# Norms of q and k in DeltaNet heads: squares by channel and a product with ones in place of transposes

## The chip, the cores and the metric

The kernel runs on one core of a Trainium2 chip. A core has five engines that run their own instruction streams and wait for each other by semaphores: TensorE (matrix products into the PSUM banks), VectorE, ScalarE, GpSimd and SyncE, which here only issues DMAs. The metric is the device time of one execution in microseconds, lower is better. The time before is the median of three runs.

## The reference

One decoder layer for 256 tokens of 2048 channels in float32. One projection `u @ w_in` feeds two token mixers, stick-breaking attention and a gated DeltaNet, each with 16 heads of 128 channels; gates merge them, and a SwiGLU network follows. The change concerns the norms of the DeltaNet's q and k:

```python
def _l2norm(x):
    return x * lax.rsqrt(jnp.sum(x * x, axis=-1, keepdims=True) + EPS)
...
qkv_b = jax.nn.silu(_causal_depthwise_conv(qkv_b, conv_w[l]))
qb, kb, vb = jnp.split(qkv_b, (D_GDN_K, 2 * D_GDN_K), axis=-1)
qb = _l2norm(_heads(qb, GDN_HEADS, GDN_K_DIM)) * (GDN_K_DIM ** -0.5)
kb = _l2norm(_heads(kb, GDN_HEADS, GDN_K_DIM))
...
o_b = _gated_delta_rule(qb, kb, vb, g, beta)
```

The delta rule solves, for each chunk and head, a unit lower triangular system made of `beta * k k^T * decay`. The kernel never writes normalised q or k: the inverse roots of the sums of squares enter as factors, by token, into that system and into the output's scaling.

## The kernel before

**Projections.** `run_jobs` walks through jobs of 512 output columns. For every 256 rows of a weight it loads a tile `raw`, makes a rounded high part `wh` (ScalarE, line 304) and the rest `wl` (VectorE, line 310), and TensorE forms three products for each part: high by high, high by low, low by high (tile `acc`). The q, k and v projections of the DeltaNet come out with channels on the partitions (`chan`), each product 256 columns wide; other projections have products 512 columns wide.

**DeltaNet chains.** The 16 heads are worked on in four groups of `HG` = 4, one chain each (`gdn_chain`). A convolution chain (`conv_chain`) makes the tiles `gq`, `gk`, `gv` (in the code `qT`, `kT`, `vT`: 128 channels by 4 heads by 256 tokens) with a Silu at its end. The tokens are worked on in two blocks of 128, the digit in the step's name. `gdn_slots` gives each step a slot in a table, and `paced` issues the TensorE part of a step at its slot and the evacuations it returns some slots later. A slot passes with each pump of the job loop, between the products of the projections. The steps that matter here:

- G and D: the decay matrix, with an Exp on ScalarE.
- K0, K1 (slots 1 and 4), T0, T1 (slots 10 and 14): four transposes each, of k or q, to have tokens on the partitions; then, one slot later, four squares on ScalarE with a sum along the channels (`accum_out`), two slots later EPS and the root on VectorE and GpSimd (`root`), two slots later the factors (`coef`, for k). K0 also copies the transposed k to `k0`, which step S0 reads at slot 53.
- KK0, KK1 (slots 7 and 13): k k^T, scaled into the system `L` with the factors. From KK1 on, the inverse of the diagonal blocks is made by substitution on VectorE (`gather`, `enter`, `stages`, `leave`), then scattered by ScalarE (`scatter`) and turned by VectorE (`turn`).
- X and Q (from slot 32): products that grow the inverse from blocks of 16 to 32 to 64, each handed between TensorE, ScalarE and VectorE. Y, W, U, S, O, R, E: the rest of the inverse, the state and the outputs, and the output scaling of the chain.

**Order.** The framework plans each engine's order from the traced program: of the work that is ready by its own estimates it takes what was written first. So projections that are written behind a step run ahead of it while it is not ready; engines then execute their orders strictly. The step X0 is written in the same slot as B1, and in the trace of the second chain it runs about 20 us behind it. PSUM has eight banks, four with the tag `acc` and four with the tag `ms`; the chain's steps take theirs from `ms` (`bank`). Tiles of the tag `h2` (five) hold the squares.

Of the kernel before, what the change touches and what calls it, by code (L numbers as in the profile page):

```python
# [11 lines left out]
AF = mybir.ActivationFunctionType  # L12
ALU = mybir.AluOpType
# [9 lines left out]
HG = 4  # L23
NG = H // HG
DFF = 5632
EPS = 1e-6
# [71 lines left out]
def body(tc, cst, x, c, w_mod, b_mod, norm1_w, w_in, q_norm_w, k_norm_w, conv_w, a_log, dt_bias,  # L98
         o_norm_w, p_a, p_b, w_out, norm2_w, w_gate, w_up, w_down, out, dbg=None):
    nc = tc.nc  # L100
    ctx = ExitStack()
    x, w_mod, b_mod, w_in, p_a, p_b, w_out, w_gate, w_up, w_down, out, conv_w = (
        t[0] for t in (x, w_mod, b_mod, w_in, p_a, p_b, w_out, w_gate, w_up, w_down, out, conv_w))
# [7 lines left out]
    def bank(name, tag="ms"):  # L111
        return ps.tile([P, 512], F32, tag=tag, name=name)
# [4 lines left out]
    def mm(o, lhsT, rhs, start=True, stop=True):  # L117
        nc.tensor.matmul(o, lhsT=lhsT, rhs=rhs, start=start, stop=stop, skip_group_check=True)  # L118

    def tt(o, a, b, op):  # L120
        nc.vector.tensor_tensor(out=o, in0=a, in1=b, op=op)  # L121

    def stt(o, a, s, b, op0, op1, **kw):
        nc.vector.scalar_tensor_tensor(out=o, in0=a, scalar=s, in1=b, op0=op0, op1=op1, **kw)  # L124

    def act(o, i, f, **kw):
        nc.scalar.activation(out=o, in_=i, func=f, **kw)

    def f32(t):
        return t.bitcast(F32)  # L130
# [4 lines left out]
    ident, ones = cs0[:, 0:P], cs0[:, P:2 * P]  # L135
# [3 lines left out]
    def tr(o, i):  # L139
        nc.tensor.transpose(o, i, ident)  # L140
# [31 lines left out]
    def rsqrt(o, i):  # L172
        nc.gpsimd.tensor_tensor(out=o, in0=i, in1=half[:, 0:o.shape[-1]], op=ALU.pow)
# [377 lines left out]
    def bc(v, n=P):  # L551
        return v.unsqueeze(2).to_broadcast([P, v.shape[1], n])

    def mid(v, n):
        return v.unsqueeze(1).to_broadcast([P, n, v.shape[1]])

    def four(b):
        return b.rearrange("p (h n) -> p h n", h=4)
# [23 lines left out]


    def gdn_slots():
        at = {"K0": 1, "K1": 4, "D0": 5, "KK0": 7, "D1": 11, "KK1": 13}
        fill = {"T0": 10, "T1": 14, "A0": 16, "B0": 22, "A1": 26, "B1": 32, "V0": 40, "V1": 44}
        out = [(t, o) for o, t in {**at, **fill}.items()] + [(0, "G0"), (6, "G1")]
        for i in range(len(LEVELS)):
            b = 13 + BD + 2 * HOP * i
            out += [(b, "X0"), (b + HOP, "Q0"), (b + LAG, "X1"), (b + LAG + HOP, "Q1")]  # L590
        b += 2 * HOP
        out += [(b, "Y0"), (b + HOP, "W0"), (b + LAG, "Y1"), (b + LAG + HOP, "W1"), (b + 2 * HOP, "U0"), (b + 3 * HOP, "S0"),
                (b + 3 * HOP + 1, "O0"), (b + 4 * HOP, "S1"), (b + 4 * HOP + 1, "R1"), (b + 5 * HOP, "U1"), (b + 6 * HOP, "O1"),
                (b + 6 * HOP + 4, "E1")]
        return sorted(out)
# [16 lines left out]
    def gdn_chain(g, tl):  # L612
        while tl.get("ready", 0) < 2:
            yield
        qT, kT, vT = (tl[n] for n in "qkv")
# [13 lines left out]
        k0 = four(wB[:, 3, 512:1024])  # L629
        rr = tp.tile([P, 2, 16], F32, tag="rr", name="rr", bufs=2)  # L630
# [6 lines left out]
        h2 = lambda n, dt=F32: four(tp.tile([P, 512], dt, tag="h2", name=n, bufs=H2))  # L637
# [3 lines left out]
        hold = {}  # L641
# [11 lines left out]
        ph = lambda b, h: b[:, h * P:(h + 1) * P]  # L653
# [60 lines left out]
        def step(op, c):  # L714
            ts = slice(c * P, (c + 1) * P)
# [3 lines left out]
            if op == "G":  # L719
                Gh, Gl = hold["G", c] = h2("Gh", F32R), h2("Gl", F32R)  # L720

                def dve(o, gx):
                    return lambda: tt(o, mid(mk["triL"], HG), bc(f32(gx)[:, c, hs]), ALU.mult)
                return [(1, dve(Gh, gth)), (2, dve(Gl, gtl))]
            if op in "KT":
                src, n0 = (kT, 8) if op == "K" else (qT, 0)
                b = bank("pb_" + op)
                for h in range(HG):
                    tr(ph(b, h), src[:, h, ts])
                n4 = slice(n0 + c * HG, n0 + (c + 1) * HG)  # L730

                def squares():
                    if op == "K" and c == 0:
                        nc.scalar.copy(out=k0, in_=four(b))
                    j = h2("sqj")
                    for h in range(HG):
                        n = n0 + c * HG + h
                        act(j[:, h], ph(b, h), AF.Square, accum_out=rr[:, 0, n:n + 1])

                def root():  # L740
                    nc.vector.tensor_scalar(out=rr[:, 0, n4], in0=rr[:, 0, n4], scalar1=EPS, scalar2=None, op0=ALU.add)
                    rsqrt(r[:, n4], rr[:, 0, n4])

                def coef():
                    if op == "K":
                        tt(brk[:, s4], beta[:, c, hs], rk[:, s4], ALU.mult)
                        stt(nbrk2[:, s4], brk[:, s4], -1.0, rk[:, s4], ALU.mult, ALU.mult)
                        if c:
                            tt(bge, nbrk2[:, 4:8], egc[:, 1, hs], ALU.mult)
                return [(1, squares), (3, root), (5, coef)]  # L750
            if op == "D":
                Gh, Gl = hold.pop(("G", c))
                b = bank("pb_d")
# [3 lines left out]
            if op == "V":  # L757
                while tl["ready"] < 3:
                    pump_conv()
                b = bank("pb_v")  # L760
# [7 lines left out]
            if op == "KK":  # L768
                b = bank("pb_kk")
# [10 lines left out]
                n = -(-(BW - 2) // BST)  # L780
# [5 lines left out]
            if op == "A":  # L786
                b = bank("pb_qk")
# [3 lines left out]
            if op == "B":  # L791
                b = bank("pb_at")
# [3 lines left out]
            if op in "XQ":  # L796
# [3 lines left out]
                b = bank("pb_" + op)[:, 0:256]  # L800
# [21 lines left out]
            if op == "Y":  # L822

                b = bank("pb_X")
# [11 lines left out]
            if op == "W":  # L836
                b = bank("pb_Q")
# [8 lines left out]
            if (op, c) == ("U", 0):  # L846
                b = bank("pb_u0")
# [7 lines left out]
            if (op, c) == ("S", 0):  # L855
                b = bank("pb_s")
# [4 lines left out]
            if (op, c) == ("O", 0):  # L861
                b = bank("pb_o0")
# [9 lines left out]
            if (op, c) == ("S", 1):  # L872
                b = bank("pb_ks")
# [8 lines left out]
            if op == "R":  # L882
                b = bank("pb_qs")
# [4 lines left out]
            if (op, c) == ("U", 1):  # L888
                b = bank("pb_u1")
# [4 lines left out]
            if (op, c) == ("O", 1):  # L894
                b = bank("pb_o1")
                for h in range(HG):
                    mm(ph(b, h), attT[:, HG + h], hold["u1"][:, h])
                o1 = hold["o"]

                def squares():  # L900
                    j = h2("sqj")
                    for h in range(HG):
                        act(j[:, h], o1[:, h], AF.Square, accum_out=sso[:, 0, HG + h:HG + h + 1])
                return [(1, lambda: tt(o1, four(b), o1, ALU.add)), (3, squares)]
# [12 lines left out]
            def apply(h):  # L917
# [7 lines left out]
                [(5 + h, apply(h)) for h in range(HG)]  # L925

        yield from paced(gdn_slots(), step)

    mk = {}
# [30 lines left out]
    for g in GROUPS:  # L960
# [8 lines left out]
        for i in range(3):  # L969
            n = "qkv"[i]  # L970
# [439 lines left out]
```

## Time and profile before

| What | Value |
|---|---|
| Median of three runs | 2052.79 us (2048.81 to 2055.16) |
| The profiled execution | 2056.12 us, span from first to last instruction 2054.1 us |
| TensorE busy | 1983.1 us, 97% |
| VectorE busy | 1386.4 us, 67% |
| ScalarE busy | 1064.9 us, 52% |
| GpSimd busy | 108.9 us, 5% |
| Mean granted TensorE clock | 0.991 |

In the profile's rows PE is TensorE's matmuls, DVE is VectorE, ACT is ScalarE, POOL is GpSimd. Matmuls are pipelined: one lasts longer than the distance to the next, so the cost of a matmul in a stream is read from the distance between two starts. L12 is line 12 of the kernel; L118 and L140 are the helpers for products and transposes, L127 that for activations. The clock is a share of TensorE's full 2.4 GHz; at 0.50 it runs at 1.2 GHz.

### The profile page before, as it was taken

Reading aid. Unit: us, or ns where it says so; the run is one execution under the profiler, and the core shown is the slowest. Engines: PE = TensorE matmul, PEld = TensorE weight load, DVE = VectorE, ACT = ScalarE, POOL = GpSimd, SP = SyncE. Lnnn points to the kernel's source line nnn. Section 1 sums busy time; section 2 is a strip of 40 time slices with the busy share of each in tenths; the row PEclk is TensorE's granted clock in tenths of the full one; section 3 lists DMA queues with packets and bytes.
Section 4 is the critical chain, followed back from the end, with each engine's and each line's share of the span. In section 5 each row is a group of like instructions: output and inputs, shape, how many; then the busy total and the mean of one; then the engine's idle time right before and its main releaser. Section 6 shows DMA issues by size and latency. Waiting matters only on the chain.

```text
span 2054.1 us, 29271 instructions
## 1 busy us (share of the span) xinstructions
PE 1983.1 (97%) x11097; PEld 1720.7 (84%) x11097; DVE 1386.4 (67%) x1846; ACT 1064.9 (52%) x1766; POOL 108.9 (5%) x141
## 2 busy tenths in 40 slices
PE   1999999999999999999999999999999999999998
PEld 1899999897888888888888888788888888888887
DVE  4986979877676667447776877676775555556554
ACT  3346676776666667443454445554455334445432
POOL 4311011010000000000000000000000000000000
PEclk9899999999999999999999999999999999999999
DMA  8995533444776675768797888587875566665564
GB/s 302 386 336 184 160 126 116 125 122 142 240 229 197 223 232 165 222 193 284 253 309 257 301 320 277 178 269 239 268 244 185 195 193 188 188 189 186 186 214 134
DMA packets 208555, 449.72 MB, mean 219 GB/s; under 512 B 16103, under 2 KB 16538, under 8 KB 207902
## 3 DMA queue, kind: packets, MB, share of 16 engines
q1 hardware_dynamic: 198910, 413.25, 62.6%
q0 software_dynamic: 9504, 34.61, 4.5%
q8 instruction: 87, 1.43, 0.3%
q14 instruction: 54, 0.44, 0.1%
HBM read 445.70 MB, written 2.10 MB: 218 GB/s over the span
## 4 chain that ended last, share of the span: by engine, by line
PE 93%; DMA 3%; DVE 2%; issue 1%; ACT 1%; POOL 0%; SPq 0%; DVEq 0%; ACTq 0%; POOLq 0%
PE acc L118 85%; DMA smod<-in_w_mod 1%; DMA crow<-in_conv_w 1%; PE pb_mod L118 1%; PE pb_Q L118 1%; DMA raw<-in_w_in 0%; PE pb_oa L118 0%; PE pb_z L118 0%; PE pb_X L118 0%; DVE wl L121 0%; PE pb_af L118 0%; DVE accb L124 0%; PE pb_o L118 0%; PE pb_u L118 0%; PE pb_tr L140 0%
## 5 line engine op out<-in xcount | busy, mean ns | idle before, releaser
L121 DVE TENSOR_TENSOR wl<-raw,wh 128x1024 fp32r<-128x1024 f32 x648 | 791.8, 1224 | 515.4 <-ACT wh L304 513.8
L304 ACT CAST wh<-raw 128x1024 fp32r<-128x1024 f32 x648 | 680.2, 1050 | 776.7 <-PE acc L118 694.9
L118 PE MATMUL acc<-u,wh 128*128 128x512 f32 x1408 | 494.8, 396 | 0.0
L118 PE MATMUL acc<-u,wl 128*128 128x256 f32 x1408 | 395.3, 281 | 0.0
L118 PEld LDWEIGHTS acc<-u,wh 128*128 128x128 f32 x1408 | 264.2, 188 | 63.1
L118 PE MATMUL acc<-wh,uh 128*128 128x512 f32 x768 | 307.1, 400 | 0.0
L118 PE MATMUL acc<-wl,uh 128*128 128x512 f32 x768 | 300.6, 391 | 0.0
L118 PE MATMUL acc<-wh,ul 128*128 128x512 f32 x768 | 300.1, 391 | 0.0
L118 PEld LDWEIGHTS acc<-u,wl 128*128 128x128 f32 x1408 | 266.1, 189 | 0.2
L118 PE MATMUL acc<-uh,wh 128*128 128x256 f32 x768 | 221.3, 291 | 1.5 <-ACT part L955 1.5
L118 PE MATMUL acc<-ul,wh 128*128 128x256 f32 x768 | 218.8, 286 | 0.0
L118 PE MATMUL acc<-uh,wl 128*128 128x256 f32 x768 | 218.7, 286 | 0.0
L118 PE MATMUL acc<-wh,ff 128*128 128x512 f32 x704 | 216.9, 389 | 0.0
L118 PEld LDWEIGHTS acc<-wl,uh 128*128 128x128 f32 x768 | 144.5, 188 | 30.8
L118 PEld LDWEIGHTS acc<-wh,ul 128*128 128x128 f32 x768 | 144.8, 189 | 27.2
L118 PEld LDWEIGHTS acc<-wh,uh 128*128 128x128 f32 x768 | 144.7, 188 | 26.8
L118 PEld LDWEIGHTS acc<-wh,ff 128*128 128x128 f32 x704 | 132.0, 188 | 27.5
L118 PEld LDWEIGHTS acc<-uh,wh 128*128 128x128 f32 x768 | 148.6, 195 | 2.6 <-ACT part L955 1.7
L118 PEld LDWEIGHTS acc<-ul,wh 128*128 128x128 f32 x768 | 148.6, 193 | 0.6
L118 PEld LDWEIGHTS acc<-uh,wl 128*128 128x128 f32 x768 | 148.0, 193 | 0.4
L118 PE MATMUL acc<-wl,ff 128*128 128x512 f32 x352 | 137.0, 389 | 0.0
L202 DVE SCALAR_TENSOR_TENSOR macc<-wm,cols,macc 128x1024 f32<-128x1024 f32 x92 | 117.7, 1280 | 0.8 <-DMA wm<-in_w_mod 0.6
(289 smaller groups left out, 2269.2 us busy)
## 6 DMA issues: line engine op xcount, KB each, us to landing
raw<-in_w_in SPq DMA_DIRECT2D x286, 512.0 KB, 4.2
wm<-in_w_mod SPq DMA_DIRECT2D x128, 512.0 KB, 5.6
raw<-in_w_gate SPq DMA_DIRECT2D x88, 512.0 KB, 4.5
raw<-in_w_up SPq DMA_DIRECT2D x88, 512.0 KB, 4.4
raw<-in_w_down SPq DMA_DIRECT2D x88, 512.0 KB, 4.3
smod<-in_w_mod POOLq DMA_DIRECT2D x64, 512.0 KB, 11.4
raw<-in_p_a SPq DMA_DIRECT2D x32, 512.0 KB, 4.9
raw<-in_p_b SPq DMA_DIRECT2D x32, 512.0 KB, 5.0
```

Of the source, the lines that this page charges most:

```text
L118: nc.tensor.matmul(o, lhsT=lhsT, rhs=rhs, start=start, stop=stop, skip_group_check=True)
L121: nc.vector.tensor_tensor(out=o, in0=a, in1=b, op=op)
L202: ins = nc.vector.scalar_tensor_tensor(out=acc, in0=t, scalar=cc[:, k:k + 1], in1=acc, op0=ALU.mult, op1=ALU.add)
L304: nc.scalar.copy(out=wh, in_=raws[n])
```

## The change

Instead of transposing k and q and squaring the transposed heads one by one, the squares are taken where the tiles lie, with channels on the partitions: one activation for four heads (new steps N0, N1 for k, M0, M1 for q). The sums over channels are made by TensorE: in steps K and T the squares of each head are the stationary side of a product with one column of ones, whose result has tokens on the partitions, one column for each head. VectorE adds EPS directly from that bank. The transposed k that K0 left for S0 is made by a step of its own, C0, at slot 36. The slots of K0 and K1 go from 1 and 4 to 2 and 5; the root comes one slot after the product, the factors two later.

```diff
-        at = {"K0": 1, "K1": 4, "D0": 5, "KK0": 7, "D1": 11, "KK1": 13}
-        fill = {"T0": 10, "T1": 14, "A0": 16, "B0": 22, "A1": 26, "B1": 32, "V0": 40, "V1": 44}
+        at = {"N0": 0, "K0": 2, "N1": 3, "K1": 5, "D0": 5, "KK0": 7, "D1": 11, "KK1": 13}
+        fill = {"M0": 8, "T0": 10, "M1": 12, "T1": 14, "C0": 36, "A0": 16, "B0": 22, "A1": 26, "B1": 32, "V0": 40, "V1": 44}
...
+            if op in "NM":
+
+                src = kT if op == "N" else qT
+                hold[op, c] = j = h2("sqj")
+                return [(1, lambda: act(j, src[:, :, ts], AF.Square))]
             if op in "KT":
-                src, n0 = (kT, 8) if op == "K" else (qT, 0)
-                b = bank("pb_" + op)
+                n0 = 8 if op == "K" else 0
+                j = hold.pop(("N" if op == "K" else "M", c))
+                b = bank("pb_n")
                 for h in range(HG):
-                    tr(ph(b, h), src[:, h, ts])
+                    mm(b[:, h:h + 1], j[:, h], ones[:, 0:1])
                 n4 = slice(n0 + c * HG, n0 + (c + 1) * HG)
 
-                def squares():
-                    if op == "K" and c == 0:
-                        nc.scalar.copy(out=k0, in_=four(b))
-                    j = h2("sqj")
-                    for h in range(HG):
-                        n = n0 + c * HG + h
-                        act(j[:, h], ph(b, h), AF.Square, accum_out=rr[:, 0, n:n + 1])
-
                 def root():
-                    nc.vector.tensor_scalar(out=rr[:, 0, n4], in0=rr[:, 0, n4], scalar1=EPS, scalar2=None, op0=ALU.add)
+                    nc.vector.tensor_scalar(out=rr[:, 0, n4], in0=b[:, 0:HG], scalar1=EPS, scalar2=None, op0=ALU.add)
                     rsqrt(r[:, n4], rr[:, 0, n4])
...
-                return [(1, squares), (3, root), (5, coef)]
+                return [(1, root), (3, coef)]
+            if op == "C":
+
+                b = bank("pb_K")
+                for h in range(HG):
+                    tr(ph(b, h), kT[:, h, ts])
+                return [(1, lambda: nc.scalar.copy(out=k0, in_=four(b)))]
```

## Rows read from the trace of the kernel before

**Rows 1.** The chain that ended last, shares of the span by engine.

```profile
PE 93%; DMA 3%; DVE 2%; issue 1%; ACT 1%; POOL 0%; SPq 0%; DVEq 0%; ACTq 0%; POOLq 0%
```

**Rows 2.** Windows: length, busy us of PE, PEld, DVE, ACT, POOL, then granted clock.

```profile
185.00:500.00 315.00, 303.26 (x2463) 286.35 (x2462) 262.74 (x622) 220.42 (x548) 31.14 (x37) 0.98 0.43 129
```

**Rows 3.** Timeline of TensorE at step X: start, us, instruction, [idle before].

```profile
243.93 0.45 PE L118 MATMUL pb_X<-gw 128*64 128x64 f32 x8 [1.42 <-issue]
244.31 0.39 PE L118 MATMUL acc<-ul,wh 128*128 128x256 f32 x1
...
329.71 0.70 PE L118 MATMUL pb_X<-gw 128*64 128x64 f32 x8 [2.88 <-ACT gw L127]
...
399.62 0.69 PE L118 MATMUL pb_X<-gw 128*64 128x64 f32 x8 [3.94 <-issue]
...
479.37 0.62 PE L118 MATMUL pb_X<-gw 128*64 128x64 f32 x8 [3.00 <-issue]
```

**Rows 4.** Windows of five microseconds from each X on.

```profile
244.00:249.00 5.00, 4.65 (x52) 4.13 (x53) 4.76 (x16) 4.57 (x13) 0.00 (x0) 1.00 0.09 35
329.70:334.70 5.00, 4.99 (x45) 4.62 (x45) 4.39 (x13) 2.91 (x7) 0.00 (x0) 0.70 0.23 63
399.60:404.60 5.00, 4.97 (x35) 4.66 (x37) 3.69 (x13) 3.50 (x8) 0.00 (x0) 0.52 0.05 17
479.40:484.40 5.00, 5.00 (x33) 3.95 (x35) 3.48 (x10) 2.50 (x5) 0.00 (x0) 0.66 0.32 87
```

**Rows 5.** Timeline of TensorE, first chain, around K0, K1 and KK0.

```profile
195.88 0.60 PE L140 MATMUL pb_K<-cs,gk 128*128 128x128 f32 x4
196.23 0.36 PE L118 MATMUL acc<-uh,wl 128*128 128x256 f32 x1
196.44 0.28 PE L118 MATMUL acc<-uh,wh 128*128 128x256 f32 x1
196.55 0.28 PE L118 MATMUL acc<-ul,wh 128*128 128x256 f32 x1
...
197.26 0.60 PE L140 MATMUL pb_K<-cs,gk 128*128 128x128 f32 x4
...
200.53 1.15 PE L118 MATMUL pb_kk<-gk 128*128 128x128 f32 x8
201.44 0.36 PE L118 MATMUL acc<-uh,wh 128*128 128x256 f32 x1
```

**Rows 6.** Timeline of VectorE: waits ahead of X in chains two to four.

```profile
296.65 0.69 DVE L121 TENSOR_TENSOR part<-acc,part 128x512 f32<-128x512 f32 x1 [0.99 <-PE acc L118]
...
362.36 0.17 DVE L741 TENSOR_SCALAR rr<-rr 128x4 f32<-128x4 f32 x1 [2.91 <-ACT sqj L127]
...
454.09 1.23 DVE L121 TENSOR_TENSOR wl<-raw,wh 128x1024 fp32r<-128x1024 f32 x1 [1.72 <-ACT wh L304]
```

**Rows 7.** Timeline of ScalarE: a cast, the squares of T1, a set for K0, a 512-wide activation.

```profile
235.88 1.05 ACT L304 CAST wh<-raw 128x1024 fp32r<-128x1024 f32 x1 [1.83 <-PE acc L118]
...
298.56 0.28 ACT L127 ACTIVATE sqj<-pb_T 128x128 f32<-128x128 f32 x1
...
439.93 0.30 ACT L127 ACTIVATE sqj<-pb_K 128x128 f32<-128x128 f32 x1
...
440.94 0.53 ACT L127 ACTIVATE gv<-acc,cw 128x256 f32<-128x256 f32 x1
...
446.66 0.63 ACT L127 ACTIVATE gv<-gv 128x512 f32<-128x512 f32 x1
447.20 1.03 ACT L304 CAST wh<-raw 128x1024 fp32r<-128x1024 f32 x1
```

**Rows 8.** Timeline of TensorE: two products of 32 and 16 columns.

```profile
185.36 0.52 PE L118 MATMUL pb_g<-gt,cs 128*128 128x32 f32 x4
185.72 0.36 PE L118 MATMUL acc<-uh,wl 128*128 128x256 f32 x1
```

**Rows 9.** Timeline of TensorE: T1 of the second chain.

```profile
294.58 0.60 PE L140 MATMUL pb_T<-cs,gq 128*128 128x128 f32 x4
```

## The prediction

> **What bounds the kernel now.** I read the chain of waits first. It gives TensorE 93% of the span and ScalarE 1% [rows 1], so most of the kernel costs what its matmul stream costs, and an edit can matter only where it changes that stream or a place where the stream stands still. The DeltaNet chains, which the change edits, run from 185 to 500 us. The windows view of that stretch [rows 2] has TensorE busy 303.3 of 315 us, VectorE 262.7, ScalarE 220.4, at a granted clock of 0.98: some 12 us of TensorE idle, and a little clock missing.
>
> The timeline of TensorE shows where both are. The four chains each have one long stop, all at the same step: the products X of the triangular inverse, with 1.42, 2.88, 3.94 and 3.00 us of idle before them, 11.2 us together [rows 3]. After the first the clock stays at 1.00; in the five microseconds after the other three it is 0.70, 0.52 and 0.66 on average [rows 4], that is, part of each at the lower of TensorE's levels (1.2 for 2.4 GHz), after an idle of 2.9 us or more. That costs 5 x (0.30 + 0.48 + 0.34) = 5.6 us. So about 17 us of this stretch are stops and their aftermath, and the rest is matmul throughput. Ahead of X, around the norms, TensorE does not stop: transposes and projections follow each other without idle [rows 5].
>
> What X waits for is a long serial piece on VectorE and ScalarE (gather, fifteen rows of substitution, scatter, turns). The timeline of VectorE tells what holds that piece back, by its last idle before X. In the first two chains it is TensorE: in the first a cast on ScalarE at 235.88, between two steps of the substitution, had waited 1.83 us for a projection to free its buffer [rows 7], and in the second VectorE waits 0.99 us at 296.65 for a projection's sum [rows 6]. In the third VectorE waits 2.91 us for the squares on ScalarE at 362.36, and its timeline shows no idle of that size between there and X; in the fourth it waits 1.72 us at 454.09 for a cast on ScalarE [rows 6].
>
> **The change, part by part.**
>
> *Transposes removed.* Four steps (K0, K1, T0, T1) in four chains, four transposes each: 64. A set of four takes 195.88 to 196.23 = 0.35 us, and the projection after it is followed by the next at 0.21 instead of 0.11 us, so a set costs 0.35 + 0.10 = 0.45 us of TensorE [rows 5]. Sixteen sets: 7.2 us removed. Four sets come back as step C0: 1.8 us. C0 stands at slot 36 and its reader S0 at slot 53; its ScalarE copy is only moved. Between X and S0 TensorE fills every gap with projections, so I cost the moved transposes at their own time and no more; if the copy landed in the X-Q-X relay it would add its own length, about 0.5 us a chain.
>
> *Products with the column of ones added.* 64 products of 128 x 128 by one column, each with the squares as weights. The trace has no one-column product, but what their f32 passes cost can be bounded. An f32 product is two records. With 128 moving columns four of them take 200.53 to 201.44 = 0.91 us, 114 ns a record [rows 5]; with 32 and 16 columns two take 0.36 us, 90 ns a record [rows 8]. A quarter of the columns hardly shortens it: the time goes with the 128 columns of weights. Where the weights have only 64 columns, four products take 243.93 to 244.31 = 0.38 us, 48 ns a record [rows 3]. I take 95 ns, close to the row with the fewest moving columns: a set of four is 8 x 0.095 + 0.10 = 0.86 us, sixteen are 13.8 us (13.1 by 90 ns, 16.2 by 114, and 7.7 by the 64-column row).
>
> The Trainium skill has two rules here, in TensorE: Matmul & The Clock Gate. Its section "Back-to-back issue gap" gives about 60 cycles for up to 64 moving columns; its section "LDWEIGHTS (loading the stationary operand)" gives the number of weight columns over 1.2 in ns, 107 ns for 128, and this rule speaks against the change. By the first, 128 records would be an estimated 3.2 us, by the second 13.7; the trace decides for the second, with 90 ns at 16 and 32 columns.
>
> TensorE's own sum: -7.2 + 1.8 + 13.8 = +8.4 us (7.7 to 10.8; +2.3 by the 64-column row). Of it (0.86 - 0.45) x 4 = 1.6 us a chain lies before X and 0.45 after.
>
> *Squares.* A set of four with its accumulator reads takes 439.93 to 440.94 = 1.01 us on ScalarE; one activation over 128 x 512 advances the engine by 446.66 to 447.20 = 0.54 us [rows 7]. Sixteen sets save 7.5 us of ScalarE, 1.9 us a chain before X, and the copy of k (about 0.5 us) moves behind X. ScalarE is not on the chain, so this is worth only what arrives at X.
>
> *Sums.* The VectorE step that adds EPS now reads TensorE's bank in place of a tile in SBUF: same count and shape, 0.17 us [rows 6], cost nothing. The root on GpSimd stays. One more bank of the tag with four is taken per chain; before, no wait of TensorE in this stretch is long enough to tell of a lack. No DMA is issued, moved or passed.
>
> *The new wait.* Before, ScalarE could be late with the squares and TensorE did not care: at T1 of the second chain the transposes begin at 294.58 [rows 9] and their squares at 298.56, 4.0 us later [rows 7]. Now TensorE's product waits for the activation, and all projections queue behind it. The activation is posted one slot ahead of its product, and a slot is about half a microsecond here (K0 and K1, three slots apart, begin at 195.88 and 197.26 [rows 5]). The squares are also issued two slots earlier than the old ones, and the set before is shorter, so I expect most products to find them ready. Below: nothing. Above: half of the 4 us at T1 and nothing elsewhere, 2 us in each chain, 8 us in all. I take 0.5 us a chain, 2 us.
>
> *What X gives back.* In the first two chains the piece before X is timed by TensorE itself, so 1.6 us more ahead of it delays X by as much: 3.3 us paid. In the third and fourth it is timed by VectorE and ScalarE, TensorE only comes to X later, and the idle takes the 1.6 us: nothing paid. Those idles fall from 3.94 and 3.00 to about 2 us and 1 us, so I also take back half of the 4.1 us that the lower clock costs after them, 2 us. Sum: 3.3 + 1.8 (C0) + 2 (waits) - 2 (clock) = +5.1 us.
>
> The profiled execution took 2056.12 us, 3.3 above the median of the three runs (2052.79), with a span of 2054.1. The sum makes that span 2059.2, and against the median it gives 2057.9: **2058 us**, 0.25% slower. A measurement of this kernel tells about 0.3% (6.2 us) from no change.
>
> **The rivals.**
>
> *Paid in full.* The planner knows of the products and puts X ahead of as many fewer projections; then the idles stay and the whole 8.4 us (to 10.8) is paid, with 0 to 8 us of waits for squares on top: 2061 to 2069, most likely 2063. For it: TensorE is the chain nearly everywhere, and an order planned on estimates keeps its idles when both sides are delayed alike. Against: in chains three and four nothing that X waits for depends on these products once they are done. It passes the 0.3% when less than 2.2 us of the 8.4 is hidden.
>
> *The lighter ScalarE arrives at X: faster.* If the 1.9 us of squares and the 0.5 us of copy per chain come off the piece before X, its idle shrinks by up to 2.4 us in each chain while TensorE comes 1.6 us later; then the three clock losses go too. 4 x 2.4 + 5.6 = 15.2 us gained against 8.4 paid: -6.8, 2046. For it: in chains three and four VectorE's last idles are on ScalarE. Against: in the first two they are on TensorE, and in the third the squares stand behind the previous chain's output scalings on ScalarE, which stay. It becomes faster by over 0.3% only if nearly all of that arrives; half of it ends near no change.
>
> *The product is cheap.* If a one-column product cost what the 64-column weights show, TensorE would pay 2.3 us, mostly hidden at X, and the relief would show: 2045 to 2053. Against: 90 ns at 16 and 32 columns. This shares the chance of the faster case.
>
> **How the numbers follow.** My forecast (half hidden, within 0.3%) 0.47; paid in full 0.38, beyond 0.3%; the faster rivals 0.15, of which 0.03 end within 0.3%. So faster 0.12, same 0.50, slower 0.38. The likeliest case alone spans 2053 to 2060. The range takes in the full price with some waits and half of the relief: 2050 to 2067.
>
> **What would show it.** In the profile after: 128 one-column records at 0.8 to 0.9 us per set of four (right), or 0.4 (the cheap rival); 16 activations of 0.5 us for 64; the idle before X at about 1.4, 2.9, 2 and 1 us (forecast), unchanged (paid in full), or gone with the clock at 1.00 after it (faster); idle before the products naming the squares (the new wait). The prediction fails if the planner places the substitution or the activation-table loads otherwise than before, for then X moves for reasons that no row here prices.

## The result and the profile after

The changed kernel takes 2064.67 us (median of 6 runs, 2061.74 to 2066.37) against 2053.43 us (6 runs of the kernel before): a ratio of 1.0055, 95% interval 1.0042 to 1.0068, 11.2 us slower. That lies within the range on record and above its likeliest value of 2058; it is the time of the rival "paid in full" (2061 to 2069). By the prediction's own mark of 0.3% it is slower, which had a chance of 0.38.

The profiled execution took 2066.37 us, its span is 2064.6 us. The difference arises in the DeltaNet stretch. The attention heads that follow it square their q from 519.9 us on, as the view of the tile `sqj` shows; in the kernel before they did so from 507.2 us on, 12.7 us earlier. At the end of the span 10.5 us of that are left; the other 2 come back far behind the change (the distance is still 12.7 us some 800 us later). The changed kernel, and behind it the same row of the kernel before:

```profile
L118 PE MATMUL pb_n<-cs,sqj x128: 164/250/352, 200.0 to 465.1; 128*128 128x1 f32 x128
L127 ACT ACTIVATE sqj<-sq x32: 295/298/314, 519.9 to 761.5; 128x128 f32<-128x128 f32 x32
...
L127 ACT ACTIVATE sqj<-gk x8: 613/622/629, 199.3 to 448.0; 128x512 f32<-128x512 f32 x8
L127 ACT ACTIVATE sqj<-gq x8: 615/620/626, 209.8 to 460.4; 128x512 f32<-128x512 f32 x8
```

```profile
L127 ACT ACTIVATE sqj<-sq x32: 293/295/308, 507.2 to 748.8; 128x128 f32<-128x128 f32 x32
```

Of the 12.7 us, 1.2 had come up before the chains began: the products that stood at 185.36 [rows 8] now stand at 186.55. About 11.5 us are the chains' own.

The change did what it says: 128 one-column records (an f32 product is two) and 16 wide activations; where two follow each other, they start 0.53 us apart (199.29 and 199.82 in the timeline of ScalarE). In the timeline of TensorE, second chain, the sets K0, T0 and T1 look like this:

```profile
292.07 0.94 PE L118 MATMUL pb_n<-cs,sqj 128*128 128x1 f32 x8
...
300.21 0.94 PE L118 MATMUL pb_n<-cs,sqj 128*128 128x1 f32 x8
301.01 0.36 PE L118 MATMUL acc<-uh,wh 128*128 128x256 f32 x1
301.21 0.28 PE L118 MATMUL acc<-ul,wh 128*128 128x256 f32 x1
...
305.30 0.95 PE L118 MATMUL pb_n<-cs,sqj 128*128 128x1 f32 x8
306.10 0.37 PE L118 MATMUL acc<-uh,wh 128*128 128x256 f32 x1
```

A set takes 300.21 to 301.01 = 0.80 us, and the projection after it again has its successor 0.20 instead of 0.12 us later. The transposes in its place took 0.35 us [rows 5]. With one column a product costs as much as with 128 (the next product K K^T of this chain starts at 297.17 and its follower at 297.97, 0.80 us too).

The first chain has something that the others have not:

```profile
198.22 0.28 PE L118 MATMUL acc<-uh,wh 128*128 128x256 f32 x1
199.97 1.05 PE L118 MATMUL pb_n<-cs,sqj 128*128 128x1 f32 x8 [1.47 <-ACT sqj L127]
...
203.02 1.70 PE L118 MATMUL pb_n<-cs,sqj 128*128 128x1 f32 x8
204.58 0.56 PE L118 MATMUL acc<-uh,wl 128*128 128x256 f32 x1
204.94 0.41 PE L118 MATMUL acc<-uh,wh 128*128 128x256 f32 x1
```

TensorE stands still for 1.47 us before the first products, until their squares are there, and the next set takes 203.02 to 204.58 = 1.56 us, twice its usual time. The timeline of ScalarE shows what the squares stood behind: a cast `wh` that itself waited 1.22 us for TensorE, and the second half of the Silu of k:

```profile
197.68 1.05 ACT L304 CAST wh<-raw 128x1024 fp32r<-128x1024 f32 x1 [1.22 <-PE acc L118]
198.63 0.62 ACT L127 ACTIVATE gk<-gk 128x512 f32<-128x512 f32 x1
199.29 1.15 ACT L127 ACTIVATE sqj<-gk 128x512 f32<-128x512 f32 x2
```

The stops before X, in the same view as [rows 3], and then windows after the first products and after each X, with the granted clock in the third column from the right:

```profile
251.95 0.45 PE L118 MATMUL pb_X<-gw 128*64 128x64 f32 x8 [2.04 <-issue]
...
341.36 0.60 PE L118 MATMUL pb_X<-gw 128*64 128x64 f32 x8 [2.75 <-ACT gw L127]
...
412.88 0.46 PE L118 MATMUL pb_X<-gw 128*64 128x64 f32 x8 [2.01 <-issue]
...
491.87 0.70 PE L118 MATMUL pb_X<-gw 128*64 128x64 f32 x8 [2.33 <-issue]
```

```profile
201.00:209.00 8.00, 8.00 (x42) 7.86 (x42) 5.00 (x14) 3.43 (x4) 2.04 (x2) 0.57 0.25 72
251.90:256.90 5.00, 4.95 (x44) 4.62 (x44) 4.62 (x15) 3.57 (x9) 0.00 (x0) 0.66 0.06 23
341.30:346.30 5.00, 4.94 (x44) 4.72 (x44) 4.55 (x17) 2.71 (x6) 0.00 (x0) 0.66 0.11 43
412.80:417.80 5.00, 4.92 (x41) 4.75 (x43) 4.19 (x12) 3.87 (x7) 0.00 (x0) 0.66 0.16 38
491.80:496.80 5.00, 4.93 (x39) 4.03 (x39) 4.17 (x13) 2.52 (x6) 0.00 (x0) 0.67 0.31 79
```

With the stop before the products the stops sum to 10.6 us, against 11.2 before [rows 3]: no gain of note. The clock takes 8 x 0.43 + 5 x (0.34 + 0.34 + 0.34 + 0.33) = 10.2 us, against 5.6 before [rows 4]. So of the 11.5 us some 4 are stops and clock together, and the rest is work: 16 sets at (0.80 + 0.08) - 0.45 = 0.43 us are 6.9 us, and C0 is to be added. The experiments take these apart.

### The profile page after: what moved, and what is told of

Read it like the earlier page. It is cut to its first block, busy times and chain, and to the rows that moved or that the text cites. A ratio compares the mean times of both kernels' runs of the same rounds, so it can differ in the third digit from the quotient of the medians.

```text
span 2064.6 us, 29323 instructions
## 1 busy us (share of the span) xinstructions
PE 1992.8 (97%) x11177; PEld 1732.7 (84%) x11177; DVE 1387.9 (67%) x1846; ACT 1059.6 (51%) x1654; POOL 109.9 (5%) x141
## 4 chain that ended last, share of the span: by engine, by line
PE 92%; DMA 3%; DVE 2%; issue 1%; ACT 1%; POOL 0%; SPq 0%; DVEq 0%; ACTq 0%; POOLq 0%
PE acc L118 84%; DMA smod<-in_w_mod 1%; DMA crow<-in_conv_w 1%; PE pb_mod L118 1%; PE pb_Q L118 1%; PE pb_n L118 1%; DVE wl L121 1%; PE pb_oa L118 0%; PE pb_z L118 0%; DMA raw<-in_w_in 0%; PE pb_X L118 0%; PE pb_af L118 0%; PE pb_o L118 0%; PE pb_kk L118 0%; PE pb_tr L140 0%
```

## The experiments

Theory A: TensorE is the chain through all of the DeltaNet stretch, and the time changes by TensorE's own work, its stops, and its clock. B: the planned order and the stops before X make the loss. C: it is waits for squares. D: what is taken off ScalarE arrives at X, and the products only ate the gain. All times are medians; ratios are to runs of the kernel before on the same chip.

**Products that wait for nothing.**

```diff
-                    mm(b[:, h:h + 1], j[:, h], ones[:, 0:1])
+                    mm(b[:, h:h + 1], ones, ones[:, 0:1])
```

> The 64 products take a constant tile of ones as weights in place of the squares, so no product waits for a square; the squares are still made and the sums are left out (each is 128). Theory A (the changed kernel loses 11.2 us to three things: the longer TensorE sets, about 0.45 us for each of 16 and not hidden in the first, second and fourth chain; the wait of the first chain's products K0 for their squares, 1.6 us; and the lower clock after that wait, about 2.5 us): the wait and its clock go, the sets stay, so about 4 us less than the changed kernel, 2060 to 2062 us. Rival B (the time is lost in the planned order and the stops before X, not at the products): unchanged, 2064 to 2066. Rival C (all the loss is waits for squares): back to 2053 to 2056.

Measured: 2056.39 us, ratio 1.0011 (1.0002 to 1.0020), twice the fall that A expected, though just short of C. The windows after X tell why:

```profile
246.80:251.80 5.00, 4.96 (x43) 4.63 (x44) 4.19 (x15) 3.35 (x9) 0.00 (x0) 0.66 0.01 3
334.10:339.10 5.00, 4.41 (x50) 4.03 (x51) 4.81 (x18) 3.60 (x8) 0.00 (x0) 1.00 0.18 66
405.80:410.80 5.00, 4.67 (x52) 4.19 (x53) 4.80 (x15) 4.66 (x11) 0.00 (x0) 1.00 0.18 41
483.60:488.60 5.00, 4.72 (x47) 3.93 (x47) 3.88 (x12) 3.61 (x10) 0.00 (x0) 1.00 0.29 70
```

The low clock is left after one X only, so some 8 us of the 10.2 are gone in this execution. The 1.5 us stop is gone, and the second chain's stop before X is 1.97 us instead of 2.75. The sets cost what they did. Over eleven executions the mean clock has a median of 0.993, against 0.990 over six of the changed kernel; a time of its own for that cannot be split off.

**Each product twice.**

```diff
                     mm(b[:, h:h + 1], j[:, h], ones[:, 0:1])
+                for h in range(HG):
+                    mm(b[:, 8 + h:9 + h], j[:, h], ones[:, 0:1])
```

> Each set of four products is made twice, the second into columns of the bank that nobody reads: 16 sets of 0.81 us more on TensorE, 13 us. Theory A: paid in full in the first two chains, 6.5 us, and in the other two beyond the stops of 2.0 and 2.3 us that are left before X, some 2 us: 8 to 11 us more than the changed kernel, 2073 to 2076 us, with shorter stops before X in the third and fourth chain. Rival B: within 3 us of the changed kernel. If all is paid: 2078.

Measured: 2078.95 us (4 runs), ratio 1.0116 (1.0102 to 1.0129), 14.3 us above the changed kernel by the medians and 12.5 by the ratios. All 13 us are paid, beyond what A expected. In the fourth chain, KK1 and X (timeline of TensorE; first before, then the changed kernel, then this one):

```profile
450.08 1.05 PE L118 MATMUL pb_kk<-gk 128*128 128x128 f32 x8
```

```profile
462.80 1.05 PE L118 MATMUL pb_kk<-gk 128*128 128x128 f32 x8
```

```profile
475.11 1.05 PE L118 MATMUL pb_kk<-gk 128*128 128x128 f32 x8
...
505.04 0.69 PE L118 MATMUL pb_X<-gw 128*64 128x64 f32 x8 [2.31 <-issue]
```

X follows KK1 after 29.3 us before [rows 3], 29.1 in the changed kernel and 29.9 with doubled products, of which T1 now takes 0.8 more in between. In the third chain the three distances are 29.7, 30.3 and 31.2 us. And the stop ahead of X is 2.33 us in the changed kernel and 2.31 with doubled products (2.01 and 1.99 in the third chain): it does not take up the work. This is where the prediction's step on X fails.

**One pass per product.** The squares are written as fp32r and multiplied with two columns of fp32r ones.

```diff
-                hold[op, c] = j = h2("sqj")
+                hold[op, c] = j = h2("sqj", F32R)
...
-                    mm(b[:, h:h + 1], j[:, h], ones[:, 0:1])
+                    mm(b[:, 2 * h:2 * h + 2], j[:, h], onesr[:, 0:2])
...
-                    nc.vector.tensor_scalar(out=rr[:, 0, n4], in0=b[:, 0:HG], scalar1=EPS, scalar2=None, op0=ALU.add)
+                    nc.vector.tensor_scalar(out=rr[:, 0, n4], in0=b[:, 0:2 * HG:2], scalar1=EPS, scalar2=None, op0=ALU.add)
```

> The squares are written as fp32r (rounded, so the sums are a little less exact) and multiplied with two columns of the fp32r ones: one record per product in place of two, so a set should take about 0.40 us in place of 0.81, 6.6 us less on TensorE. Theory A: the first, second and fourth chain give 1.6 us each back, the third little, the wait in the first stays: 4.5 to 6.5 us less, 2058 to 2060 us. Rival B: 2064 to 2066. Rival C: 2064 to 2066.

Measured: 2056.30 us, ratio 1.0008 (0.9999 to 1.0017), 8.4 us below the changed kernel, more than A expected. A set is now as short as the transposes were:

```profile
293.36 0.50 PE L118 MATMUL pb_n<-rmask,sqj 128*128 128x2 f32 x4
293.72 0.36 PE L118 MATMUL acc<-uh,wh 128*128 128x256 f32 x1
```

0.36 for 0.80 us, 7.0 us over 16 sets. The squares are still waited for in the first chain (1.47 us in this execution too), but no lower clock follows that stop, which in the changed kernel took 3.4 us. So the fall is the shorter sets and some clock together.

**K0 and K1 later in the first chain.**

```diff
+        if g == 0:
+            at.update(K0=5, K1=7)
```

> In the first chain alone K0 goes from slot 2 to 5 and K1 from 5 to 7; nothing else. Theory A: the squares are ready when the first products are reached, the stop of 1.6 us and the lower clock from 202 to 208 us go: 3 to 4 us less, 2061 to 2062 us, and no stop of TensorE before the first chain's products. Rival B: unchanged or moved by what happens before X, 2064 to 2066. A variant of A, that the stop only moves to KK0 or X because the system then starts later: 2063 to 2065.

Measured: 2060.49 us, ratio 1.0026 (1.0018 to 1.0035), 4.2 us below the changed kernel, as A had it, but not for A's reason: the stop is still there, 1.31 us before the first products. The products start at 199.73, in the changed kernel at 199.97: three slots more did not move them, as the planner goes by its own estimates. What differs in this execution is the clock, which stays up after that stop and is low after two X only. The run says nothing about the wait alone.

**No wait at K0 of the first chain alone.**

```diff
-                    mm(b[:, h:h + 1], j[:, h], ones[:, 0:1])
+                    mm(b[:, h:h + 1], ones if (g, op, c) == (0, "K", 0) else j[:, h], ones[:, 0:1])
```

> The changed kernel with one difference: the four products of K0 in the first chain take constant ones as weights, so the one product that TensorE was seen to wait for no longer waits (those sums are left out). TensorE's work is unchanged. Theory A: the stop of 1.5 us before those products goes and with it the lower clock right after, 1.5 to 5 us less than the changed kernel, 2060 to 2063; the rest, some 9 us of work, stays, so not under 2058. Rival C (the loss is the wait): 2053 to 2056.

Measured: 2060.47 us, ratio 1.0027 (1.0019 to 1.0036), against 1.0055: 4.2 us less by the medians, 5.8 by the ratios. In place of 1.47 us TensorE now waits 0.41, for the squares of K1, and the windows there are at full clock:

```profile
200.18 1.05 PE L118 MATMUL pb_n<-cs,sqj 128*128 128x1 f32 x8 [0.41 <-ACT sqj L127]
```

```profile
198.00:203.00 5.00, 4.59 (x38) 4.34 (x37) 4.12 (x12) 4.77 (x7) 2.04 (x2) 1.00 0.55 142
203.00:208.00 5.00, 5.00 (x44) 4.91 (x43) 4.77 (x15) 4.95 (x7) 0.53 (x1) 1.00 0.26 73
```

In this execution the clock also stays up after the first X, 1.7 us that need not be due to the wait; the shorter stop and the clock right behind it are 1.1 and 3.4 us.

**The lighter ScalarE alone, on the kernel before.**

```diff
-                        act(j[:, h], ph(b, h), AF.Square, accum_out=rr[:, 0, n:n + 1])
+                        pass
+                    act(j, four(b), AF.Square)
+                    hold['j', op, c] = j
...
-                    nc.vector.tensor_scalar(out=rr[:, 0, n4], in0=rr[:, 0, n4], scalar1=EPS, scalar2=None, op0=ALU.add)
+                    nc.vector.tensor_scalar(out=rr[:, 0, n4], in0=hold['j', op, c][:, 0, 0:HG], scalar1=128.0, scalar2=None, op0=ALU.add)
```

> The kernel before with one change: the squares of four transposed heads are one 512-wide activation from the bank, and their sums are left out (the root gets four of the squares plus 128). TensorE's work and every wait stay as before; ScalarE has 7.5 us less in all, 1.9 us a chain ahead of X. Theory A (the time is TensorE's own work, its stops and its clock, and X follows TensorE at a fixed distance from KK1): within 2 us of before. Rival D (what is taken off ScalarE arrives at X, and the change's gain was eaten by the products): 4 to 8 us less than before, 2046 to 2050.

Measured: 2054.60 us against 2055.01, ratio 0.9994 (0.9986 to 1.0003). 7.5 us off ScalarE are worth nothing that can be told, and the stops before X sum to 11.1 us for 11.2 [rows 3] (the first is 1.42 as before):

```profile
330.91 0.45 PE L118 MATMUL pb_X<-gw 128*64 128x64 f32 x8 [2.72 <-ACT gw L127]
...
401.88 0.70 PE L118 MATMUL pb_X<-gw 128*64 128x64 f32 x8 [4.43 <-issue]
...
481.28 0.45 PE L118 MATMUL pb_X<-gw 128*64 128x64 f32 x8 [2.50 <-issue]
```

D falls.

**C0 alone, on the kernel before.**

```diff
+"C0": 36
...
-                    if op == "K" and c == 0:
-                        nc.scalar.copy(out=k0, in_=four(b))
...
+            if op == "C":
+                b = bank("pb_K")
+                for h in range(HG):
+                    tr(ph(b, h), kT[:, h, ts])
+                return [(1, lambda: nc.scalar.copy(out=k0, in_=four(b)))]
```

> The kernel before with step C0 alone: K0 no longer copies, and the transposed k is made a second time at slot 36 for S0. 16 more transposes. Theory A: 0.45 us a chain, up to twice that where the clock is low after X, 2 to 3 us more than before. Rival: hidden in the gaps of the relay after X, within 1 us of before; or the copy lands in the relay and costs 0.5 us a chain more, 4 us.

Measured: 2056.20 against 2055.01 us, ratio 1.0003 (0.9995 to 1.0012): about 1 us, with anything from -1 to 2.5 possible. The 1.8 us of the sum and the lower part of A's 2 to 3 stay within the interval, 4 us do not.

**Neither long products nor waits.**

```diff
-                    mm(b[:, h:h + 1], j[:, h], ones[:, 0:1])
+                    mm(b[:, 2 * h:2 * h + 2], onesr, onesr[:, 0:2])
```

> The one-pass products take constant ones (fp32r) as weights, so neither the length of the products nor the wait for the squares is left; the sums are left out. With either cause alone removed the time fell by 8.3 and 8.4 us of the 11.2 lost. Theory A: TensorE has only C0 more than before (1.8 us), the two causes share what the clock took, so they do not add up: 2052 to 2056. If the two are independent, the falls add up: 2048. Rival B (order and stops): 2056, as with either alone.

Measured: 2052.85 against 2055.01 us, ratio 0.9988 (0.9979 to 0.9996). The two falls do not add up: by the ratios they are 9.0 us (no wait) and 9.7 us (one pass), and together 13.8 (1.0055 to 0.9988). That fits A, by which they share what the clock took; the run does not show it by itself.

**A mixed kernel.** K0 keeps its transposes, which are needed for `k0` anyhow, with its four squares; C0 and N0 go; K1, T0 and T1 take the one-pass products. In the slots K0 is back at 1; the branch for K0 is the old one.

```diff
-        at = {"N0": 0, "K0": 2, "N1": 3, "K1": 5, "D0": 5, "KK0": 7, "D1": 11, "KK1": 13}
+        at = {"K0": 1, "N1": 3, "K1": 5, "D0": 5, "KK0": 7, "D1": 11, "KK1": 13}
...
+            if (op, c) == ("K", 0):
+                b = bank("pb_K")
+                for h in range(HG):
+                    tr(ph(b, h), kT[:, h, ts])
```

> K0 stays as it was before, with transposes that also give k0, and C0 goes; K1, T0 and T1 take the products of the changed kernel with fp32r squares, one record each. A set of transposes and a set of one-pass products both take 0.36 us of TensorE, so its work is that of before; ScalarE has 5.6 us less; the first chain's wait for squares is at K1 only. Theory A: 2 us either side of before, most likely 1 to 2 us less, 2052 to 2054. Rival D: 4 us or more less than before. If the products cost something that their records do not show: 2056 to 2060.

Measured: 2052.77 against 2055.01 us, ratio 0.9988 (0.9979 to 0.9996). It is the best version here beside the one above, which leaves the sums out, by 0.04 to 0.21% against the kernel before. In its execution the stops before X are 2.04, 1.73, 2.11 and 2.29 us, 8.2 in all for 11.2 [rows 3], but two more of 0.88 and 1.25 us, before K0 of the first chain and a product of the third, make it 10.3; the low clock follows one X only.

**The mixed kernel with the products of the change.** The same with `j` in F32 and one column of `ones`, so two records per product.

```diff
-                    mm(b[:, 2 * h:2 * h + 2], j[:, h], onesr[:, 0:2])
+                    mm(b[:, h:h + 1], j[:, h], ones[:, 0:1])
```

> The mixed kernel (K0 by transposes, which also give k0; no C0; K1, T0, T1 by products) with the products of the change, two records each. Against the mixed kernel with one-pass products only the 12 sets differ, 0.81 for 0.36 us: 5.4 us of TensorE. Theory A: paid in full, 2052.8 + 5.4 = 2058, between 2057 and 2060. Rival (stops before X take the sets of the third and fourth chain): 2055 to 2056.

Measured: 2056.77 against 2054.03 us, ratio 1.0010 (1.0001 to 1.0020). The step from 0.9988 to 1.0010 is 4.5 us for 12 sets that are 0.45 us longer each, 5.4 us; given the two intervals, the rival's half of that is possible too. The two profiled executions decide: from K0 of the first chain to X of the fourth it is 281.7 us with one-pass products (196.55 to 478.21) and 286.7 with these (194.55 to 481.20), 5.0 us more, with the low clock in between after the first X alone in both. The stops before X are 1.97 and 2.25 us in the third and fourth chain for 2.11 and 2.29. So the products are paid nearly in full, where C0 and a wait of K0 for wide squares play no part.

## Why the prediction was right or wrong

**Products: right.** 0.86 us a set was expected with its tail, 0.88 measured; of the sum of +8.4 us for TensorE's work some 8 are paid. The trace has 0.80/8 = 100 ns a record at one column, and the rival "the product is cheap" falls with it. By the rule in the Trainium skill's page TensorE: Matmul & The Clock Gate, section "LDWEIGHTS (loading the stationary operand)", 128 weight columns are an estimated 107 ns, and the trace agrees within 7 ns. The 60 cycles for so few columns in that page's section "Back-to-back issue gap" are given there for a product by itself; of a stream in which each product loads weights the section says that both steps set the spacing, and the 100 ns bear that out.

**What X gives back: this step failed.** It said that in the third and fourth chain X is timed by VectorE and ScalarE, so that TensorE comes later to it and the idle takes 1.6 us a chain, and half of the clock's loss with it. It rested on VectorE's last idle [rows 6]: a wait for squares or for a cast, taken to be independent of TensorE. The runs show otherwise. X keeps its distance to KK1, a TensorE product that stands behind three of the four sets, and that distance does not shrink when the sets are doubled.

The timeline of VectorE shows how this comes about. Before, its longest waits in these two chains named ScalarE [rows 6]. In the changed kernel, fourth chain, the last long ones name TensorE: KK1, and the product of q and k behind T1 (`pb_qk`). With doubled products, below, the second of them is 0.76 us longer:

```profile
463.96 0.87 DVE L124 SCALAR_TENSOR_TENSOR gw<-pb_kk,co,gw 128x128 f32<-128x128 f32 x3 [0.94 <-PE pb_kk L118]
...
467.74 0.69 DVE L121 TENSOR_TENSOR gw<-pb_qk,gw 128x512 f32<-128x512 f32 x1 [1.45 <-PE pb_qk L118]
```

```profile
476.26 0.87 DVE L124 SCALAR_TENSOR_TENSOR gw<-pb_kk,co,gw 128x128 f32<-128x128 f32 x3 [0.93 <-PE pb_kk L118]
...
480.94 0.69 DVE L121 TENSOR_TENSOR gw<-pb_qk,gw 128x512 f32<-128x512 f32 x1 [2.21 <-PE pb_qk L118]
```

From that step to X it is 24.13 us in the changed kernel and 24.10 with doubled products, of which VectorE is busy 22.7 in both. So X is timed by VectorE, as the prediction said, but VectorE's piece begins when TensorE gets to these products, and the longer sets delay that. With lighter squares on the kernel before, VectorE's waits are taken over by the next in line, in the third chain by a cast that stands behind output scalings on ScalarE, in the fourth by KK1:

```profile
363.44 1.23 DVE L121 TENSOR_TENSOR wl<-raw,wh 128x1024 fp32r<-128x1024 f32 x1 [2.35 <-ACT wh L304]
...
453.66 1.12 DVE L124 SCALAR_TENSOR_TENSOR gw<-pb_kk,co,gw 128x128 f32<-128x128 f32 x4 [1.52 <-PE pb_kk L118]
```

That this is the path by which X follows TensorE is read from these rows, for the fourth chain; what is tested is that X follows. Two stops did fall, 3.94 to 2.01 us in the third chain and 3.00 to 2.33 in the fourth. They are 2.0 and 2.3 us there with single, doubled and one-pass products alike, so this comes with the new order and not with a later arrival of TensorE; which part of the order does it stays open. (The forecast's own figures of about 2 and 1 us are also 0.3 to 0.4 us lower than 3.94 and 3.00 less 1.64.)

**The new wait: its size about right, its place and its price wrong.** 2 us were taken, 0.5 in each chain, with T1 as the place for more; it came once, at K0 of the first chain, 1.47 us, because the squares stand behind a Silu and a cast that waits for TensorE. What the prediction did not price is the clock after it: 3.4 us in the profiled execution. The run without that one wait is 4.2 to 5.8 us faster; 1.7 us of that may be clock behind another stop.

**The clock after X: wrong sign.** 2 us were to come back; 10.2 us were lost in place of 5.6, as the low clock followed all four X and the new stop. That is the profiled execution, whose mean clock of 0.989 is the lowest of the six. Two of the six had 0.992, with spans of 2060.0 and 2060.4; the executions of the kernel before at that clock, in the three groups that the experiments were compared with, average 2051.9 to 2052.5. At 0.991 it is 2062.6 (one execution) against 2053.0 to 2053.4. So 8 to 10 us are lost where the mean clock is the same, and the clock adds 1 to 3 at the median.

**C0 and the lighter ScalarE: right.** About 1 us was measured for 1.8, which its interval allows, and nothing for 7.5 us of ScalarE; the rival on the other side falls with the latter.

So the time is that of the rival "paid in full", and its main claim holds: the planned order keeps the stops before X, and TensorE's work is paid. By the terms of the sum, against the profiled execution: TensorE's work +8.4 forecast, some 8 measured (6.9 for the sets and about 1 for C0); stops -1.3 forecast (2 of new waits less 3.3 given back), -0.6 measured; clock -2 forecast, +4.6 measured. These make +11.9 against the 11.5 us found, where the forecast had 5.1. Most of the miss is thus the clock, the last part of the step on X. By the executions at the same clock, too, it is 3 to 5 of the 6 us by which the medians miss the sum (11.2 for 5.1). The hiding failed as a mechanism; that the stops before X fell by 2.1 us all the same, of the 3.3 forecast, is luck, as they fell for another reason. The time lies within the range because the range took in the price of the rival, not because the forecast's mechanism held.

## What to carry to other kernels

A sum over partitions by a product with one column is not a small product: its weights are the data, and their columns, not the moving ones, set its time (100 ns a record here, against 48 with 64 columns of weights and more moving columns [rows 3]), so weigh it by records times about 0.1 us against the transposes it replaces; a rounded one-pass operand (fp32r) more than halved it here, 0.36 for 0.80 us. Where an engine is the chain on both sides of a stop, a stop is no reserve: ask by what distance the waiting step follows work of the same engine, and not only which engine was late last. A consumer that is moved from a lenient engine's queue to the bounding engine's queue can turn a lateness of its producer into a stop, and the clock can make that stop cost more than its length (here 1.47 us, and 3.4 in the profiled execution).

## What the hardware showed that was not expected

The lower clock (1.2 in place of 2.4 GHz) does not go by the length of the stop ahead of it alone. Before, 1.42 us was followed by full clock, and 2.88 by 0.70 on average over 5 us [rows 3, 4]. In the changed kernel 1.47 us was followed by 0.57 on average over 8 us, while the one-pass kernel had the same stop of 1.47 us and kept full clock. Products that wait for nothing had stops of 2.06, 1.97, 2.01 and 2.31 us before X, and only the first was followed by the lower clock (0.66 over 5 us). From execution to execution of the changed kernel the mean clock moves between 0.989 and 0.992, and the spans with it, 2064.6 and 2060.0 to 2060.4 us. What decides was not found, so the clock's part of the loss is known only as a few microseconds.
